# Score products of an item first, transposes three and value products four items behind

## Chip, cores and metric

The kernel runs on one core of one Trainium2 chip. The metric is the device time of one execution in microseconds; the median of 3 runs of the kernel before is 2927.72 us (2925.48 to 2929.70).

## What is computed

One step of a hybrid decoder layer, for a prompt of 2048 tokens and for 8 short sample sequences of 4 tokens with a cache. The change touches the prompt's dilated attention alone. There are 8 heads of 64 dims. Each query attends to itself and 128 keys behind it, in three patterns (stride 1, 4 and 16), and the three outputs are merged afterwards by their log-sum-exp.

```python
# prompt branch for one dilation, cut: 128-query blocks, each against its own and the previous key block
kb = jnp.concatenate([kp[:, :-1], kp[:, 1:]], axis=2)
scores = jnp.einsum('bnqchd,bnkchd->bnchqk', qb, kb).astype(jnp.float32) * (HEAD_DIM ** -0.5)
bias = -slopes[:, None, None] * (dilation * diff).astype(jnp.float32)[None]
scores = jnp.where(valid[None, :, None, None], scores + bias[None, None, None], NEG)
m = jnp.max(scores, axis=-1, keepdims=True)
p = jnp.exp(scores - m)
l = jnp.sum(p, axis=-1, keepdims=True)
out = jnp.einsum('bnchqk,bnkchd->bnqchd', (p / l).astype(v.dtype), vb)
```

Before it come the input projection with norms, after it the output projection, the gated feed-forward part and, beside that, the attention of the samples. All of these are unchanged.

## The kernel before

The program has stages: the input projection of the prompt in 16 tiles of 128 tokens, the prompt attention, the merge with the output projection, and the up and down projections in four chunks of 512 tokens. The attention's first 8 items run at the end of the first stage; the other 184 run in a loop of their own (lines 720 to 739) with an order written out by hand: each engine gets its instructions in the order in which the program issues them.

**An item** is (head h, pattern p, pair pr): two of the 16 query blocks of one head in one pattern. A head has 24 items (3 patterns of 8 pairs). A query block, here called a half of the item, has one or two key blocks of 128: it is 128 or 256 columns wide. Stride 16 has one key block everywhere, stride 4 has two from its fifth query block on, stride 1 from its second. The two items (p, 2n) and (p, 2n+1) come in a row, and the patterns take turns.

**Three steps of an item.** `scores` (line 275) multiplies each half's queries with the keys' high and low parts (lines 289 and 290) into one PSUM bank `Sp`, of which there are four. Then line 292 adds the bias table on VectorE, with the row's minimum into `st` (scores carry a minus sign), and line 294 takes the exponential on ScalarE into `Pt`. `turn` (line 298) transposes the item's two to four blocks of `Pt` on TensorE (line 302) into a PSUM bank `tp` and copies them to `PTs`, three times of four on VectorE (line 305), else on ScalarE (line 307). `values` (line 311) multiplies `PTs` with the values and a column of ones into the bank `Op`, two instructions per block (line 324). Every second item ScalarE copies `Op` to `O` (line 328); after four items of a pattern POOL adds `st` (line 330) and, once both heads of a pair are done, SP stores `O` to DRAM.

**The order.** `advance(i)` (line 356) issues `scores` of item i, `turn` of item i-2 and `values` of item i-3. In `scores` the first half's products, its line 292 and line 294 come ahead of the second half's products. POOL copies queries into the order of a pattern (`spread_q`, line 241) six items ahead.

**Loads.** `load_head` (line 243) loads a head's queries and keys into `QK`, two buffers, in six DMAs of 512 KB on SP's queue (lines 161 to 166), and POOL makes the head's bias table `tab`. It is issued in the loop when item 4 of the head before begins. `next_v` takes one of six `V` buffers, for (pair of heads, pattern, half of the blocks); POOL sets its ones columns (lines 176 and 177) and SP loads it (lines 185 and 193). `NEXT_V` (line 718) says at which items. SP's queue also carries the stores of `O`, small rows of parameters (line 205) and, from item 150 on, eight tiles `rawo` of the output projection's weight (line 737), which ScalarE and VectorE split into a high and a low part (lines 112 and 113).

Of the kernel before, what the change touches and what calls it, by code (L numbers as in the profile page):

```python
# [9 lines left out]
F32 = mybir.dt.float32  # L10
# [7 lines left out]
P = 128  # L18
# [3 lines left out]
H = 8  # L22
# [25 lines left out]
def kernel(ctx, tc, ins, cst, outs):  # L48
# [173 lines left out]
    def store_o(p, hp, O, half):  # L222

        eng = nc.gpsimd if hp == 3 and p == 0 and half else nc.sync
        dst = o_s[p * S:(p + 1) * S, hp, :]
        if p == 0:
            eng.dma_start(dst.rearrange("(n i) f -> i n f", i=P)[:, 8 * half:8 * half + 8], O)
        elif p == 1:
            for J in range(2):
                J2 = 2 * half + J  # L230
                eng.dma_start(dst[J2 * CH:(J2 + 1) * CH].rearrange("(i c) f -> i c f", c=4), O[:, 4 * J:4 * J + 4, :])
        else:
            eng.dma_start(dst.rearrange("(i c) f -> i c f", c=16)[:, 8 * half:8 * half + 8], O)
# [27 lines left out]
    def views(h, p, idx):  # L261
        r = DILS[p]
        blk, c = divmod(idx, r)
        lo = blk - 1 if blk else 0

        def keys(x):
            if p == 0:
                return x[:, lo * P:(blk + 1) * P]
            return x.rearrange("p (m c i) -> p m c i", c=r, i=RUN)[:, lo * P // RUN:(blk + 1) * P // RUN, c, :]

        return queries(h, p, idx), keys(heads[h][1]), keys(heads[h][2]), ([idx - r] if blk else []) + [idx]
# [3 lines left out]
    def scores(it):  # L275
        h, p, pr = it
        tab = heads[h][3]
        if pr % 4 == 0:
            state["st", p] = pq.tile([P, 8], F32, tag="st", name="st", bufs=8)
        st = state["st", p]  # L280
        Sp = psum.tile([P, 2, 2 * P], F32, tag="mm", name="Sp", bufs=4)
        Pt = pq.tile([P, 2, 2 * P], F32, tag="P", name="Pt", bufs=3)
        blocks = []
        for s in range(2):
            idx = 2 * pr + s
            i8 = idx % 8
            q, kh, kl, kb = views(h, p, idx)
            w = P * len(kb)
            nc.tensor.matmul(Sp[:, s, :w], q, kh, start=True, stop=False)  # L289
            nc.tensor.matmul(Sp[:, s, :w], q, kl, start=False, stop=True)  # L290
            T = pq.tile([P, 2 * P], F32, tag="T", name="T", bufs=3)
            nc.vector.tensor_tensor_reduce(out=T[:, :w], in0=Sp[:, s, :w], in1=tab[:, p, 2 * P - w:], op0=ALU.add,  # L292
                                           op1=ALU.min, scale=1.0, scalar=3e38, accum_out=st[:, i8:i8 + 1])
            nc.scalar.activation(Pt[:, s, :w], T[:, :w], AF.Exp, bias=st[:, i8:i8 + 1], scale=-1.0)  # L294
            blocks += [(s, idx % 4, n, b, len(kb)) for n, b in enumerate(kb)]
        return st, Pt, blocks

    def turn(it, res):
        st, Pt, blocks = res
        tp = psum.tile([P, 4, P], F32, tag="tp", name="tp2", bufs=4)  # L300
        for j, (s, i4, n, b, m) in enumerate(blocks):
            nc.tensor.transpose(tp[:, j, :], Pt[:, s, n * P:(n + 1) * P], ident)  # L302
        PT = pq.tile([P, 4, P], F32, tag="PTs", name="PTs", bufs=4)
        if evac[0] % 4:
            nc.vector.tensor_copy(PT[:, :len(blocks)], tp[:, :len(blocks)])
        else:
            nc.scalar.copy(PT[:, :len(blocks)], tp[:, :len(blocks)])
        evac[0] += 1
        return PT

    def values(it, res, PT):
        h, p, pr = it
        hp, h2 = divmod(h, 2)
        st, Pt, blocks = res
        half, pr4 = divmod(pr, 4)
        if h2 == 0 and pr4 == 0 and (p, half) not in pair_o:
            pair_o[p, half] = p2.tile([P, 8, OW], F32, tag="O", name="O", bufs=6)
        O = pair_o[p, half]
        if pr % 2 == 0:
            state["Op", p] = psum.tile([P, 4, DH + 1], F32, tag="tp", name="Op", bufs=4)  # L320
        Op = state["Op", p]
        v0 = h2 * (DH + 1)
        for j, (s, i4, n, b, m) in enumerate(blocks):
            nc.tensor.matmul(Op[:, i4, :], PT[:, j, :], pair_v[hp, p, b][:, v0:v0 + DH + 1],  # L324
                             start=n == 0, stop=n == m - 1)
        o0 = h2 * (DH + 2)
        if pr % 2:
            nc.scalar.copy(O[:, 2 * pr4 - 2:2 * pr4 + 2, o0:o0 + DH + 1], Op)
        if pr4 == 3:
            nc.gpsimd.tensor_copy(O[:, :, o0 + DH + 1], st)  # L330
            if h2 == 1:
                store_o(p, hp, O, half)
                del pair_o[p, half]
# [3 lines left out]
    def turns(seq):  # L337
        at = {}
        for p in seq:
            n = at[p] = at.get(p, -1) + 1  # L340
            yield from ((p, 2 * n), (p, 2 * n + 1))

    ORDER = [(0, 0, 0, 0) + (2, 1) * 4] + [(0, 2, 1) * 4] * (H - 2) + [(0, 2, 2, 1, 2, 0, 2, 1, 0, 1, 1, 0)]
    items = [(h, p, pr) for h in range(H) for p, pr in turns(ORDER[h])]
    NI = 24
    AHEAD = 8
    SPREAD = 6
    attn, PTs = {}, {}

    def spread_next(i):  # L350
        if i < len(items):
            h, p, pr = items[i]
            if p and pr % 2 == 0:
                spread_q(h, p, pr // 2)

    def advance(i):
        if i >= AHEAD:
            spread_next(i + SPREAD)
        if i < len(items):
            attn[i] = scores(items[i])  # L360
        if 0 <= i - 2 < len(items):
            PTs[i - 2] = turn(items[i - 2], attn[i - 2])
        if 0 <= i - 3 < len(items):
            values(items[i - 3], attn.pop(i - 3), PTs.pop(i - 3))


    right = ExitStack()
# [1 line left out]
    with tc.tile_pool(name="p1", bufs=1) as p1:  # L369
# [295 lines left out]
        pq = right.enter_context(tc.tile_pool(name="pq", bufs=1, side="right", reuse_waits="tile"))  # L665
# [17 lines left out]
        for i in range(AHEAD):  # L683
            advance(i)
# [8 lines left out]
    def h_tile(k):  # L693

        return ph.tile([P, 2, TM], F32R, tag=f"h{k}", name="h", bufs=1)
# [14 lines left out]
    with tc.tile_pool(name="p2", bufs=1, reuse_waits="tile") as p2:  # L710
        wo0 = [h_tile(k) for k in range(KT)]
        for half in range(2):
            for p in (2, 1):
                next_v(0, p, half)
        nc.vector.memset(stT[:, :, 2 * SB:], 0.0)
        for i in range(AHEAD, AHEAD + SPREAD):
            spread_next(i)
        NEXT_V = {(1, 14): (2, 0), (1, 17): (0, 0), (1, 21): (1, 0), (1, 23): (0, 1), (0, 1): (2, 1), (0, 3): (1, 1)}

        with tc.manual_schedule():  # L720
            for i in range(AHEAD, len(items) + 3):
                if i < len(items):
                    h, li = divmod(i, NI)
                    if (i == AHEAD or h and li == 4) and h + 1 < H:
                        load_head(h + 1)

                    if (h % 2, li) in NEXT_V and 0 < h < H - (h % 2):
                        next_v((h + 1) // 2, *NEXT_V[h % 2, li])
                    j, r = divmod(i - NI, 8)
                    if r == 0 and 0 <= j < 15:  # L730
                        param_load(j)
                    if r == 5 and 0 < j < 16:
                        param_turn(j - 1)
                    if i >= 150 and i % 5 == 0 and i < 190:
                        k = ((i - 150) // 5 + 4) % KT
                        raw = p2.tile([P, CH], F32, tag="row", name="rawo", bufs=2)
                        nc.sync.dma_start(raw, wov[:, k, 0:CH])
                        split(wo0[k][:, 0, 0:CH], wo0[k][:, 1, 0:CH], raw)
                    if (h, li) == (7, 0):
                        mBs[0] = load_pool(0)  # L740
                advance(i)
# [3 lines left out]
    with tc.tile_pool(name="p4", bufs=1, reuse_waits="tile") as p4:  # L745
# [102 lines left out]
        for gi, grp in enumerate(groups):  # L848
# [22 lines left out]
            for i, t in enumerate(grp):  # L871
# [4 lines left out]
                if i >= late and nxt:  # L876
                    n = nxt[i - late]
# [243 lines left out]
        for c in range(NCHUNK):  # L1121
            last = c == NCHUNK - 1
            T = TM if last else CH
            spans = [(0, T // 2), (T // 2, T // 2)] if last else [(0, CH)]
            nt = 5 if last else 4

            def spread(pss, prompt, sample):

                if not last:
                    return [(prompt, pss[0])]  # L1130
                h = T // 2
                return [(prompt[:, 0:h], pss[0][:, :h]), (prompt[:, h:CH], pss[1][:, :CH - h]),
# [52 lines left out]
            def up_pair(i, slot, act):  # L1185
                gt = conv_tile(i)
                vt = conv_tile(NF + i)
                sg = p4.tile([P, TM], F32, tag="cv", name="sg", bufs=4)
                nc.scalar.activation(sg[:, :T], gt[:, :T], AF.Silu)
                nc.vector.tensor_tensor(out=vt[:, :T], in0=vt[:, :T], in1=sg[:, :T], op=ALU.mult)  # L1190
# [102 lines left out]
```

## Time and profile before

| what | value |
|---|---|
| median of 3 runs | 2927.72 us |
| profiled execution | 2930.08 us |
| its span | 2928.3 us |
| TensorE matmul busy | 2762.1 us (94%) |
| TensorE weight load busy | 2355.7 us (80%) |
| VectorE busy | 1750.5 us (60%) |
| ScalarE busy | 1108.0 us (38%) |
| GpSimd busy | 184.3 us (6%) |
| granted TensorE clock, mean over the span | 0.874 |
| DMA | 393.60 MB, 134 GB/s over the span |

The prompt attention's loop lies between about 466 and 1176 us of the span. In the rows below, PE is TensorE's matmul, PEld its weight load, DVE VectorE, ACT ScalarE, POOL GpSimd; L289 is line 289. Matmuls are pipelined and a row's end is modelled, so the pace of matmuls is read from start to start, not from the length of one row. A few matmul records are missing from a trace. [...]

### The profile page before, as it was taken

Reading aid. Unit: us, or ns where it says so; the run is one execution under the profiler, and the core shown is the slowest. Engines: PE = TensorE matmul, PEld = TensorE weight load, DVE = VectorE, ACT = ScalarE, POOL = GpSimd, SP = SyncE. Lnnn points to the kernel's source line nnn. Section 1 sums busy time; section 2 is a strip of 40 time slices with the busy share of each in tenths; the row PEclk is TensorE's granted clock in tenths of the full one; section 3 lists DMA queues with packets and bytes.
Section 4 is the critical chain, followed back from the end, with each engine's and each line's share of the span. In section 5 each row is a group of like instructions: output and inputs, shape, how many; then the busy total and the mean of one; then the engine's idle time right before and its main releaser. Section 6 shows DMA issues by size and latency. Waiting matters only on the chain.

```text
span 2928.3 us, 36228 instructions
## 1 busy us (share of the span) xinstructions
PE 2762.1 (94%) x13310; PEld 2355.7 (80%) x13310; DVE 1750.5 (60%) x3819; ACT 1108.0 (38%) x2021; POOL 184.3 (6%) x246
## 2 busy tenths in 40 slices
PE   7999997888888687999999999999999999999999
PEld 5888887777777676787788888888888888999998
DVE  6444453333333233676889887888888766666665
ACT  5333333333333233222533434544444444444442
POOL 1111121111011110100000000000000000000000
PEclk9999996555555555999999999999999999999999
DMA  6333335332223411797855565344564344522221
GB/s 201 112 125 112 105 109 146 87 90 45 78 56 81 105 40 37 260 315 251 246 186 176 168 206 183 109 134 144 184 193 129 117 128 140 179 82 87 88 84 58
DMA packets 412877, 393.60 MB, mean 134 GB/s; under 512 B 16347, under 2 KB 319543, under 8 KB 410012
## 3 DMA queue, kind: packets, MB, share of 16 engines
q1 hardware_dynamic: 412476, 390.48, 43.6%
q8 instruction: 105, 1.72, 0.2%
q0 software_dynamic: 224, 0.80, 0.1%
q14 instruction: 72, 0.59, 0.1%
HBM read 305.70 MB, written 85.52 MB: 134 GB/s over the span
## 4 chain that ended last, share of the span: by engine, by line
PE 88%; DVE 4%; issue 3%; DMA 3%; POOL 1%; SPq 0%; ACT 0%; DVEq 0%; POOLq 0%; ACTq 0%
PE pu L1037 34%; PE pd L1213 17%; PE ps L470 11%; PE Op L324 7%; PE po L816 5%; PE Sp L289 5%; PE tp L302 4%; PE Sp L290 3%; DVE T L292 2%; PE tp L122 1%; PE tp L479 1%; PE pd L1207 1%; DMA rawo<-in_w_out_dram 1%; DMA QK<-kT_lo 1%; PE pp L551 0%
## 5 line engine op out<-in xcount | busy, mean ns | idle before, releaser
L1037 PE MATMUL pu<-h,w 128*128 128x512 f32 (+1 forms) x5232 | 990.6, 350 | 2.1 <-ACT w L112 1.6
L1037 PEld LDWEIGHTS pu<-h,w 128*128 128x128 f32 x5232 | 851.0, 188 | 133.4 <-ACT w L112 2.0
L1213 PE MATMUL pd<-w,act 128*128 128x512 f32 x2112 | 490.2, 392 | 0.0
L1213 PEld LDWEIGHTS pd<-w,act 128*128 128x128 f32 x2112 | 396.6, 188 | 88.1
L112 ACT CAST w<-raw 128x1024 fp32r<-128x1024 f32 (+1 forms) x282 | 287.0, 1026 | 292.2 <-PE pd L1213 186.2
L292 DVE CUSTOM_DVE_ANT_0 T<-Sp,tab 128x256 f32<-128x256 f32 (+1 forms) x384 | 140.1, 366 | 421.6 <-PE Sp L290 414.2
L113 DVE TENSOR_TENSOR w<-raw,w 128x1024 fp32r<-128x1024 f32 (+1 forms) x278 | 328.9, 1186 | 24.9 <-ACT w L112 24.8
L470 PE MATMUL ps<-W_hi,xh 128*128 128x512 f32 x1024 | 333.0, 398 | 1.0 <-ACT xh L112 1.0
L294 ACT ACTIVATE Pt<-T,st 128x256 f32<-128x256 f32 (+1 forms) x384 | 176.6, 462 | 411.4 <-DVE st L292 411.4
L1181 DVE SCALAR_TENSOR_TENSOR cv<-ex,cw,cv 128x512 f32<-128x512 f32 x352 | 262.3, 745 | 28.9 <-ACT cv L1173 26.3
L324 PEld LDWEIGHTS Op<-V,PTs 128*128 128x128 f32 x1200 | 273.0, 326 | 0.1
L324 PE MATMUL Op<-V,PTs 128*128 128x65 f32 x1200 | 269.2, 394 | 0.0
L1171 ACT COPY ex<-pu 128x512 f32<-128x512 f32 (+1 forms) x220 | 110.1, 500 | 345.4 <-PE pu L1037 345.2
L470 PEld LDWEIGHTS ps<-W_hi,xh 128*128 128x128 f32 x1024 | 192.7, 189 | 43.2 <-ACT xh L112 1.5
L470 PE MATMUL ps<-W_lo,xh 128*128 128x512 f32 x512 | 202.7, 396 | 0.0
L289 PE MATMUL Sp<-QK,qs 128*128 128x128 f32 (+1 forms) x256 | 128.9, 504 | 74.4 <-DVE st L292 74.4
L1215 DVE TENSOR_TENSOR ya<-ya,pd 128x512 f32<-128x512 f32 x192 | 131.0, 684 | 103.3 <-PE pd L1213 102.6
L95 POOL TENSOR_TENSOR rs<-ms,mhalf 128x8 f32<-128x8 f32 (+3 forms) x68 | 76.4, 1124 | 1588.9 <-DVE stT L1174 1048.8
L302 PE MATMUL tp<-ident,Pt 128*128 128x128 f32 x600 | 166.0, 415 | 0.0
L1173 ACT ACTIVATE cv<-pu,cw 128x512 f32<-128x512 f32 (+3 forms) x264 | 166.0, 649 | 0.0
L289 PEld LDWEIGHTS Sp<-QK,qs 128*128 128x128 f32 x256 | 78.7, 308 | 104.1 <-DVE st L292 103.7
L289 PE MATMUL Sp<-QK 128*128 128x256 f32 (+1 forms) x128 | 69.6, 550 | 61.3 <-DVE st L292 56.7
(225 smaller groups left out, 2905.9 us busy)
## 6 DMA issues: line engine op xcount, KB each, us to landing
raw<-in_w_up_dram SPq DMA_DIRECT2D x176, 512.0 KB
raw<-in_w_down_dram SPq DMA_DIRECT2D x80, 512.0 KB
hn_s<-w SPq DMA_DIRECT2D x16, 1024.0 KB
h<-hn_s SPq DMA_DIRECT2D x32, 512.0 KB
far<-in_cache_k_dram SPq DMA_DIRECT2D x64, 256.0 KB
far<-in_cache_v_dram SPq DMA_DIRECT2D x64, 256.0 KB
om<-o_s SPq DMA_DIRECT2D x16, 792.0 KB
raw<-in_w_in_dram SPq DMA_DIRECT2D x16, 512.0 KB
```

Source lines behind the costliest of these rows:

```text
L112: nc.scalar.copy(hi, src)
L113: (eng or nc.vector).tensor_tensor(out=lo, in0=src, in1=f32(hi), op=ALU.subtract)
L289: nc.tensor.matmul(Sp[:, s, :w], q, kh, start=True, stop=False)
L292: nc.vector.tensor_tensor_reduce(out=T[:, :w], in0=Sp[:, s, :w], in1=tab[:, p, 2 * P - w:], op0=ALU.add, op1=ALU.min, scale=1.0, scalar=3e ...
L294: nc.scalar.activation(Pt[:, s, :w], T[:, :w], AF.Exp, bias=st[:, i8:i8 + 1], scale=-1.0)
L302: nc.tensor.transpose(tp[:, j, :], Pt[:, s, n * P:(n + 1) * P], ident)
L324: nc.tensor.matmul(Op[:, i4, :], PT[:, j, :], pair_v[hp, p, b][:, v0:v0 + DH + 1], start=n == 0, stop=n == m - 1)
L470: nc.tensor.matmul(ps, xh[:, a, k, :], (W_hi, W_lo)[b][j, k // 2][:, k % 2, :], start=n == 0, stop=n == 3 * KT - 1)
L1037: nc.tensor.matmul(ps[:, :n], w[:, a, k, :], hs[k][:, b, c0:c0 + n], start=i == 0, stop=i == 3 * KT - 1)
L1173: nc.scalar.activation(d, s, AF.Identity, bias=cw[:, 3, ct:ct + 1], scale=cw[:, 2, ct:ct + 1])
L1181: nc.vector.scalar_tensor_tensor(out=d, in0=e[j], scalar=cw[:, j, ct:ct + 1], in1=d, op0=ALU.mult, op1=ALU.add)
L1213: nc.tensor.matmul(ps, act[0][:, a, k, tau * P:(tau + 1) * P], wd[k][:, b, :], start=k == 0 and j == 0, stop=k == n - 1 and j == 2)
```

## The change

In `scores`, all four products of an item are issued first, for both halves, and the VectorE and ScalarE steps of the two halves follow. `turn` comes three items behind `scores` in place of two, `values` four in place of three. `Pt` has four buffers in place of three and `PTs` three in place of four. The loop runs one turn longer, and `load_head` and the entries of `NEXT_V` move by one item.

```diff
-        Pt = pq.tile([P, 2, 2 * P], F32, tag="P", name="Pt", bufs=3)
-        blocks = []
+        Pt = pq.tile([P, 2, 2 * P], F32, tag="P", name="Pt", bufs=4)
+        blocks, parts = [], []
         for s in range(2):
             idx = 2 * pr + s
-            i8 = idx % 8
             q, kh, kl, kb = views(h, p, idx)
             w = P * len(kb)
             nc.tensor.matmul(Sp[:, s, :w], q, kh, start=True, stop=False)
             nc.tensor.matmul(Sp[:, s, :w], q, kl, start=False, stop=True)
+            parts.append((s, idx % 8, w))
+            blocks += [(s, idx % 4, n, b, len(kb)) for n, b in enumerate(kb)]
+        for s, i8, w in parts:
             T = pq.tile([P, 2 * P], F32, tag="T", name="T", bufs=3)
             nc.vector.tensor_tensor_reduce(out=T[:, :w], in0=Sp[:, s, :w], in1=tab[:, p, 2 * P - w:], op0=ALU.add,
                                            op1=ALU.min, scale=1.0, scalar=3e38, accum_out=st[:, i8:i8 + 1])
             nc.scalar.activation(Pt[:, s, :w], T[:, :w], AF.Exp, bias=st[:, i8:i8 + 1], scale=-1.0)
-            blocks += [(s, idx % 4, n, b, len(kb)) for n, b in enumerate(kb)]
...
-        PT = pq.tile([P, 4, P], F32, tag="PTs", name="PTs", bufs=4)
+        PT = pq.tile([P, 4, P], F32, tag="PTs", name="PTs", bufs=3)
...
-        if 0 <= i - 2 < len(items):
-            PTs[i - 2] = turn(items[i - 2], attn[i - 2])
         if 0 <= i - 3 < len(items):
-            values(items[i - 3], attn.pop(i - 3), PTs.pop(i - 3))
+            PTs[i - 3] = turn(items[i - 3], attn[i - 3])
+        if 0 <= i - 4 < len(items):
+            values(items[i - 4], attn.pop(i - 4), PTs.pop(i - 4))
...
-        NEXT_V = {(1, 14): (2, 0), (1, 17): (0, 0), (1, 21): (1, 0), (1, 23): (0, 1), (0, 1): (2, 1), (0, 3): (1, 1)}
+        NEXT_V = {(1, 15): (2, 0), (1, 18): (0, 0), (1, 22): (1, 0), (0, 0): (0, 1), (0, 2): (2, 1), (0, 4): (1, 1)}
...
-            for i in range(AHEAD, len(items) + 3):
+            for i in range(AHEAD, len(items) + 4):
...
-                    if (i == AHEAD or h and li == 4) and h + 1 < H:
+                    if (i == AHEAD or h and li == 5) and h + 1 < H:
                         load_head(h + 1)
```

## Rows read from the trace of the kernel before

**Rows 1.** The page's 40 slices of the span, granted TensorE clock in tenths.
```profile
PEclk9999996555555555999999999999999999999999
```
**Rows 2.** Table of stretches: length, busy (instructions) by engine, clock, DMA share, GB/s.
```profile
466.10:1176.10 710.00, 580.42 (x2480) 532.98 (x2480) 222.65 (x898) 224.28 (x516) 85.94 (x148) 0.50 0.28 70
511.00:1022.00 511.00, 420.08 (x1798) 385.29 (x1797) 157.54 (x641) 157.83 (x362) 66.67 (x119) 0.50 0.32 78
```
**Rows 3.** Waits in 466.1 to 1176.1 us: total us, times, longest.
```profile
ACT Pt L294 <- DVE st L292: 397.6, 368, 2.8
...
PE Sp L289 <- DVE st L292: 130.4, 184, 15.1
```
**Rows 4.** Timeline, one item with four blocks: start, us, work, [idle before <- releaser].
```profile
1154.00 0.58 PE L289 MATMUL Sp<-QK,qs 128*128 128x256 f32 x1 [0.62 <-DVE st L292]
...
1154.38 0.42 PE L290 MATMUL Sp<-QK,qs 128*128 128x256 f32 x1
...
1154.60 1.05 PE L302 MATMUL tp<-ident,Pt 128*128 128x128 f32 x4
...
1155.44 1.81 PE L324 MATMUL Op<-V,PTs 128*128 128x65 f32 x8
...
1157.01 0.56 PE L289 MATMUL Sp<-QK,qs 128*128 128x256 f32 x1
...
1157.37 0.41 PE L290 MATMUL Sp<-QK,qs 128*128 128x256 f32 x1
...
1158.42 0.58 PE L289 MATMUL Sp<-QK,qs 128*128 128x256 f32 x1 [0.63 <-DVE st L292]
```
**Rows 5.** Timeline, the scores of an item with 128-wide halves.
```profile
553.86 0.41 PE L290 MATMUL Sp<-QK,qs 128*128 128x128 f32 x1
554.77 0.47 PE L289 MATMUL Sp<-QK,qs 128*128 128x128 f32 x1 [0.50 <-DVE st L292]
555.04 0.41 PE L290 MATMUL Sp<-QK,qs 128*128 128x128 f32 x1
```
**Rows 6.** Groups by form, 466.1 to 1176.1 us: 128-wide first products with spread queries.
```profile
L289 PE MATMUL Sp<-QK,qs 128*128 128x128 f32 x159 | 73.9, 465 | 43.0 <-DVE st L292 43.0
```
**Rows 7.** Timeline at the attention's head: products in a row, low clock.
```profile
446.42 1.19 PE L289 MATMUL Sp<-QK 128*128 128x128 f32 x4 [3.01 <-DMA QK<-kT_hi]
...
450.92 0.41 PE L289 MATMUL Sp<-QK 128*128 128x256 f32 x1
451.14 0.41 PE L290 MATMUL Sp<-QK 128*128 128x256 f32 x1
451.35 1.05 PE L302 MATMUL tp<-ident,Pt 128*128 128x128 f32 x4
```
**Rows 8.** Timeline at the attention's end: the same steps at the high clock.
```profile
1176.45 0.28 PE L290 MATMUL Sp<-QK 128*128 128x256 f32 x1
1176.57 0.60 PE L302 MATMUL tp<-ident,Pt 128*128 128x128 f32 x4
1177.01 1.00 PE L324 MATMUL Op<-V,PTs 128*128 128x65 f32 x8
1177.85 0.60 PE L302 MATMUL tp<-ident,Pt 128*128 128x128 f32 x4
```
**Rows 9.** Table of stretches around the changes of the clock.
```profile
445.70:452.40 6.70, 5.22 (x20) 4.38 (x21) 1.78 (x10) 1.69 (x5) 0.00 (x0) 0.50 1.06 322
452.40:455.90 3.50, 3.50 (x18) 3.29 (x18) 1.46 (x7) 1.80 (x5) 0.00 (x0) 0.50 0.50 158
456.00:461.40 5.40, 5.40 (x51) 5.34 (x48) 3.21 (x13) 3.46 (x8) 2.13 (x11) 1.00 0.76 170
461.40:466.10 4.70, 1.72 (x10) 1.13 (x8) 1.84 (x7) 0.67 (x2) 2.48 (x3) 1.00 0.90 224
1171.70:1176.00 4.30, 4.30 (x18) 4.20 (x19) 0.83 (x4) 1.81 (x4) 0.00 (x0) 0.50 0.02 4
```
**Rows 10.** Timeline of ScalarE: its longest wait in the loop.
```profile
1014.47 0.62 ACT L112 CAST h<-rawo 128x512 fp32r<-128x512 f32 x1 [14.21 <-DMA rawo<-in_w_out_dram]
```

## The prediction

> **What bounds the kernel now.** I read the profile from the top down. The slices come first: the granted TensorE clock is 0.5 in the stretch that holds the prompt attention and 0.9 or more nearly everywhere else [rows 1]. [...] TensorE is busy for 580 us of it, VectorE for 223, ScalarE for 224 and the DMA engines for 0.28 of the time [rows 2]. So TensorE sets the end of this stage, with 130 us of idle time. The waits name all of it: line 289 waits for `st` of line 292, 184 times, which is once per item, 130.4 us in all [rows 3]. The timeline of one item with four blocks shows the place. The second half's first product follows the first half's last product by 1.05 us (1157.37 to 1158.42), because it writes the bank that VectorE is still reading for the first half. Then four transposes and eight value products run with nothing in front of them, up to the next item's first half. The item's period is 4.42 us (1154.00 to 1158.42) [rows 4]. Items with 128-wide halves have the same wait, 0.91 us start to start [rows 5].
>
> **Products first.** Four score products go out with no VectorE step between them. What a product costs without the wait stands at the head of the attention, where the program happened to issue them in a row: 0.22 us for 256 columns and, for 128 columns, (1.19 - 0.47)/3 = 0.24 us [rows 5, 7].
> - 256 wide: 1.05 falls to 0.22, and the step from line 289 to 290 falls from 0.38 to 0.22 [rows 4, 7]: 0.99 us per item.
> - 128 wide: 0.91 falls to 0.24 and 0.27 to 0.24 [rows 5, 7]: 0.70 us per item.
> - Of the 128-wide first products with spread queries there are 159, two per item, so about 80 items [rows 6]; the other 104 of 184 count as wide.
>
> Together 104 x 0.99 + 80 x 0.70 = 159 us at the low clock. Nothing of this is hidden elsewhere: TensorE is the engine that ends last. Of the 130.4 us of idle time about 25 us are other stalls (130.4 - 104 x 0.62 - 80 x 0.50), the longest 15.1 us [rows 3 to 5]; they stay.
>
> **What the first T waits for.** Line 292 of the first half now waits for the second half's two products too, since they write its bank: 0.43 us later. Queued behind it on VectorE are the second T and the eviction of the transposes; behind those, ScalarE's two exponentials. Nobody on TensorE needs them in that item: the transposes take the item three before, the value products the one four before. A whole item (3.4 us at the low clock) lies between. I cost it at nothing; without that cover it is 0.43 x 184 = 79 us.
>
> **The distances and buffers.** `Pt` gets one more buffer and `PTs` one fewer. The slot that an exponential writes was read by transposes one item earlier, as before. The pipeline empties one item later: 0 to 3.4 us, and I take 0, since the next stage's products stand ready in that place. The V loads come one item later and so does their use: nothing. `load_head` comes one item later and its use does not. That moves six 512 KB loads on SP's queue, the table on POOL in front of the query copies, and every load queued behind, `rawo` among them. Bounds: 0 to 3.4 us for each of six heads, 20 us. I take 0 at the low clock, because SP runs ahead of the item loop and a head lasts 93 us (710/7.67). The one stall of this kind, 14.21 us in front of `rawo` behind six QK loads, stays [rows 10].
>
> **The clock.** The low level is the larger prize, and the trace tells how it is left. It rose twice in this mix of work: at 455.9, after 3.5 us in which TensorE was busy for 3.50, and at 1176.0, after 4.3 us with 4.30 busy; the same engine with 5.22 of 6.70 us busy stayed at 0.50. In between it held 1.00 for 5.4 us of attention items without idle time and was lost only after 461.4, when TensorE was busy for 1.72 of 4.70 us [rows 9]. In the 710 us the short wait of each item stands between such stretches. The change takes out just that wait, so I expect the clock to rise early in the stage and to fall only at a long stall.
> The prices at the high level are in the trace: 0.12 us per wide product against 0.22, 0.44 us per four transposes against 0.84, 0.84 us per eight value products against 1.57 [rows 4, 7, 8]: a factor of 0.54. The stage without waits and stalls is 710 - 159 - 25 = 526 us at the low level; times 0.54 that is 284, and with the 25 us of stalls 309 us.
> Then transfers come next. In 511 to 1022 us the DMA engines work 0.32 x 511 = 164 us [rows 2]; at the high level that stretch lasts 511/710 x 309 = 222 us. Three quarters of the time is a tight fit for a queue that issues in order, and QK loads have a fixed deadline per head. The nearest row for one late load is the 14.21 us behind a whole head's QK [rows 10]. I take a third, 5 us, per head, and 5 us more for each stall because the clock drops and comes back only after some 10 us at half pace (445.7 to 455.9) [rows 9]: 10 x 7.67 = 77 us. The bounds are 0 and twice that, 150 us.
> [...]
>
> **The sum.** The profiled execution took 2930.1 us (span 2928.3, 1.8 around it), 2.4 above the median, so I count from it. High clock: 2930 - 710 + 309 + 77 = 2606, less the 2 us to the median: **2604 us**. Its own range is 2527 (no new stall) to 2680 (150 us of them).
>
> **Rivals.**
> - *The clock stays low.* The waits go and nothing else. For it: the clock stayed at 0.50 through 184 items with 2 to 3.6 us of unbroken work in each, and no item with 128-wide halves stands ahead of either rise. Against it: rows 9. Time 2928 - 159 = **2769**, up to 2790 with the 20 us of late QK loads.
> - *The clock comes and goes.* DMA stalls knock it down again and again, and it is up for about half of the work: (2604 + 2769)/2, about **2690**.
> - *Nothing changes.* The order does not do what it says, and the wait reappears in front of the first product or the transposes, at the same length: **2928**. Against: four `Sp` banks are free for four items.
> - *Slower: the ring of `Pt` is one short.* If an exponential had to wait for transposes that themselves stand behind the current item's scores, TensorE would wait in each item for both T chains, 2 x 0.83 us, where it saved 0.86 on average: + 0.8 x 184 = 147 us, **3075**. It decides from a new wait of over 0.86 us (159/184) per item. Against: the slack is one item before and after, and in 368 waits of line 294 the releaser is VectorE alone, never TensorE [rows 3].
>
> **How the numbers follow.** High clock for most of the stage 0.60; comes and goes 0.18; low 0.17; no change 0.02; slower 0.03. The first two hold 0.78, so the range has to reach into the third: 2530 to 2785. A difference of 0.2%, about 6 us, is what a measurement of this kernel can tell from none. Faster by more 0.95, within 0.02, slower 0.03.
>
> **What would show it.** Right: the wait of line 289 for `st` is gone from the waits, the stage's granted clock is near 1, four products stand in a row at 0.12 us. VectorE's T starts only after the fourth product. The waits left in front of TensorE are few and long and lead to a DMA (QK, V, `rawo`), each followed by a piece at 0.5. Wrong on the clock: the stage is dense and still at 0.50, some 550 us long. Wrong on the transfers: the stage is 310 us long, or above 450 at a high clock. Wrong on the whole: transposes or value products show a wait of the item's own length for `Pt` or `PTs`.

## The result

The changed kernel takes 2565.68 us (median of 4 runs, 2562.88 to 2568.02), the kernel before 2926.66 us (4 runs): a ratio of 0.8765, 95% interval 0.875 to 0.878, 361 us less. The forecast was 2604 us, in a range of 2530 to 2785.

The slices of the profile after, granted TensorE clock in tenths (compare [rows 1]):

```profile
PEclk9999999999978999999999999999999999999999
```

The nine slices at 5 are gone. The waits of TensorE in the attention loop, 460.6 to 812.6 us (total us, times, longest; compare [rows 3]). In this kernel the score products stand in lines 288 and 289, the bias step in 294, the exponential in 296, the transposes in 303, their copies in 306 and 308, the value products in 325.

```profile
PE Op L325 <- DVE PTs L306: 31.3, 5, 24.6
PE Sp L288 <- DMA QK<-kT_hi: 6.1, 1, 6.1
PE Op L325 <- ACT PTs L308: 5.9, 14, 1.8
PE Sp L289 <- DMA QK<-kT_lo: 1.9, 1, 1.9
PE tpc L217 <- DMA row<-in_state_ffn_conv_dram: 1.7, 1, 1.7
```

No score product waits for `st`. Of the 46.9 us that are left, 24.6 are one stall, another 4.7 a second one behind the same loads, and 8.0 belong to the first keys of head 1. The table of stretches after (columns as in [rows 2]):

```profile
460.60:812.60 352.00, 304.57 (x2482) 292.45 (x2481) 197.75 (x901) 195.06 (x514) 88.86 (x150) 0.91 0.59 143
498.90:649.00 150.10, 145.81 (x1247) 139.62 (x1246) 95.34 (x442) 94.45 (x250) 43.89 (x79) 1.00 0.68 161
708.70:733.30 24.60, 0.03 (x1) 0.00 (x0) 1.72 (x7) 1.21 (x3) 0.01 (x1) 0.54 0.84 193
819.70:2564.50 1744.80, 1732.76 (x8638) 1457.41 (x8637) 1303.42 (x2400) 709.86 (x1177) 21.40 (x22) 1.00 0.51 161
```

The loop, with the same 2480 or so recorded matmuls, went from 710 to 352 us; its clock is 0.91 in place of 0.50, with a piece of 150 us at 1.00 throughout. From the last value product to the end it is 1744.8 us, against 1746.6 before. So of the 364 us by which the span is shorter, 358 lie in the loop; the other 5.5 lie ahead of it (it begins at 460.6 us in place of 466.1). The scores of an item, in the timeline after (compare [rows 4 and 8]):

```profile
483.36 0.37 PE L288 MATMUL Sp<-QK,qs 128*128 128x256 f32 x1
483.56 0.29 PE L289 MATMUL Sp<-QK,qs 128*128 128x256 f32 x1
483.69 0.28 PE L288 MATMUL Sp<-QK,qs 128*128 128x256 f32 x1
483.80 0.27 PE L289 MATMUL Sp<-QK,qs 128*128 128x256 f32 x1
483.92 0.38 PE L303 MATMUL tp<-ident,Pt 128*128 128x128 f32 x2
...
484.22 0.42 DVE L294 CUSTOM_DVE_ANT_0 T<-Sp,tab 128x256 f32<-128x256 f32 x1 [0.42 <-PE tp L303]
```

Four products take 0.56 us (483.36 to 483.92), and the first bias step starts only after the fourth of them, at 484.22.

### The profile page after: what moved, and what is told of

Same layout as the page of the kernel before. It is cut to its first block, busy times and chain, and to the rows that moved or that the text cites. A ratio compares the mean times of both kernels' runs of the same rounds, so it can differ in the third digit from the quotient of the medians.

```text
span 2564.5 us, 35986 instructions
## 1 busy us (share of the span) xinstructions
PE 2483.7 (97%) x13310; PEld 2113.6 (82%) x13310; DVE 1724.9 (67%) x3819; ACT 1078.5 (42%) x2021; POOL 185.9 (7%) x246
## 4 chain that ended last, share of the span: by engine, by line
PE 66%; DMA 1%; DVE 1%; issue 0%; ACT 0%; SPq 0%; POOL 0%; DVEq 0%; ACTq 0%; POOLq 0%
PE pu L1038 38%; PE pd L1214 19%; PE po L817 5%; PE pd L1208 1%; PE tp L122 0%; DMA raw<-in_w_out_dram 0%; PE Op L325 0%; DMA h<-hn_s 0%; DMA raw<-in_w_up_dram 0%; PE sacc L990 0%; PE sacc L989 0%; PE po L1071 0%; DVE at L796 0%; PE tpa L802 0%; DMA om<-o_s 0%
## 5 line engine op out<-in xcount | busy, mean ns | idle before, releaser
L296 ACT ACTIVATE Pt<-T,st 128x256 f32<-128x256 f32 (+1 forms) x384 | 157.0, 456 | 137.4 <-DVE st L294 136.7
L294 DVE CUSTOM_DVE_ANT_0 T<-Sp,tab 128x256 f32<-128x256 f32 (+1 forms) x384 | 125.3, 364 | 122.0 <-PE Sp L289 93.3
L325 PE MATMUL Op<-V,PTs 128*128 128x65 f32 x1200 | 167.1, 278 | 38.1 <-DVE PTs L306 31.3
L325 PEld LDWEIGHTS Op<-V,PTs 128*128 128x128 f32 x1200 | 155.9, 199 | 48.7 <-DVE PTs L306 33.9
L112 ACT CAST act<-cv 128x512 fp32r<-128x512 f32 x88 | 54.6, 621 | 159.4 <-DVE cv L1191 152.6
L471 PEld LDWEIGHTS ps<-W_lo,xh 128*128 128x128 f32 x512 | 96.7, 189 | 19.9
L1175 DVE COPY stT<-ex 128x2 f32<-128x2 f32 x176 | 28.8, 163 | 117.1 <-ACT ex L1172 117.0
L303 PE MATMUL tp<-ident,Pt 128*128 128x128 f32 x600 | 102.9, 284 | 0.0
```

The lines of the kernel that those rows point to most:

```text
L112: nc.scalar.copy(hi, src)
L471: nc.tensor.matmul(ps, xh[:, a, k, :], (W_hi, W_lo)[b][j, k // 2][:, k % 2, :], start=n == 0, stop=n == 3 * KT - 1)
```

## Experiments

**Which part does it.** The first run takes the product order alone, the second the distances alone.

```diff
# e1_products_only: the kernel before, but in scores
+            parts.append((s, idx % 8, w))
+        for s, i8, w in parts:
             T = ...            # bias step and exponential of both halves, after all four products
# e2_distance_only: the changed kernel, but in scores the bias step and the exponential
# stand inside the loop over the halves, as before
```

> The kernel before with one part of the change: the four products of an item first. Distances (two and three), buffers and the places of the loads as before. Theory A (the wait between the two halves' products holds the clock down, and taking it out is the whole gain): the granted clock of the attention loop rises to 0.9 or more, the loop falls from 710 to some 350 to 380 us, 2566 to 2600 us. Theory B (the longer distances are needed, since transposes two items behind then wait for their exponentials): a new wait of line 302 for line 294 appears, 0.2 to 0.6 us per item, the clock stays at 0.50, 2770 to 2830 us.

> The changed kernel with the old order inside scores: distances three and four, buffers and loads as changed, but each half's bias step and exponential stand right behind its two products. Theory A: the wait of line 289 for st stays at about 130 us, the clock at 0.50, the time within 6 us of the 2927 before. Theory B (the distances bring the gain): 2566 to 2700 us.

The first takes 2564.59 us, ratio 0.8757 (0.8744 to 0.877), the whole gain; the second 2929.03 us, ratio 1.0004 (0.9994 to 1.0013), nothing that can be measured. Loop and waits of the first, then of the second:

```profile
461.50:811.00 349.50, 303.80 (x2479) 293.65 (x2479) 197.90 (x900) 195.03 (x514) 88.01 (x149) 0.91 0.60 144
PE Op L325 <- ACT PTs L308: 30.7, 16, 25.4
PE Op L325 <- DVE PTs L306: 9.1, 5, 5.1
```

```profile
466.70:1176.20 709.50, 580.36 (x2481) 532.76 (x2481) 223.12 (x897) 223.14 (x514) 85.75 (x148) 0.50 0.29 70
PE Sp L289 <- DVE st L292: 130.1, 184, 18.6
```

With distances of two and three no transpose waits for its exponential, so theory B falls on both sides. The longer distances, the buffers and the moved loads are worth nothing measurable.

**Is it the order of the products, or the idle time?** In the kernel before, the transposes and value products were put between the two halves, so that the bias step runs behind them. Inside an item the two halves' products are apart; the second half's products and the next item's first ones now follow each other, in two banks.

```diff
             nc.scalar.activation(Pt[:, s, :w], T[:, :w], AF.Exp, bias=st[:, i8:i8 + 1], scale=-1.0)
+            if s == 0:
+                between()      # turn of item i-2, values of item i-3; in advance they are gone
```

> The kernel before in everything but the order on the queues: transposes and value products stand between the first and the second half's products, so that the bias step of the first half runs behind them. Distances two and three, buffers and loads as before. Theory A (idle time on TensorE is what counts, in whatever way it is filled): the wait for st is nearly gone, the clock rises, 2566 to 2640 us. Theory G (four products in a row are needed for the clock): clock 0.50, only the waits' 105 us saved, 2800 to 2825 us.

2573.32 us, ratio 0.8792 (0.8779 to 0.8806). Loop and waits:

```profile
462.70:828.40 365.70, 322.36 (x2487) 313.39 (x2488) 206.23 (x897) 204.20 (x516) 87.30 (x148) 0.87 0.56 137
PE Sp L289 <- DVE st L292: 35.9, 9, 22.9
PE Sp L289 <- DMA QK<-kT_hi: 3.4, 1, 3.4
```

The 184 waits have become 9, and the clock is up. Theory A holds: another filling of the same gap gives nearly the same time. Theory G, by which four products in a row are needed, does not fall by this run: four still stand in a row, two of one item and two of the next.

```profile
561.55 0.36 PE L289 MATMUL Sp<-QK 128*128 128x256 f32 x1
561.76 0.28 PE L290 MATMUL Sp<-QK 128*128 128x256 f32 x1
561.88 0.23 PE L289 MATMUL Sp<-QK,qs 128*128 128x128 f32 x1
561.95 0.27 PE L290 MATMUL Sp<-QK,qs 128*128 128x128 f32 x1
```

The run e8_transposes_between, below, settles it.

**How much idle time holds the clock down.** Two runs leave part of it in: the whole wait in every second item, and a shortened wait in each item whose transposes do not cover it.

```diff
# e3_every_second_item: the changed kernel
+            if pr % 2 == 0:
+                finish(parts.pop())    # bias step and exponential at once, as before
+        for part in parts:
+            finish(part)
# e8_transposes_between: the kernel before
+            if s == 0:
+                between()              # turn of item i-2 only; values stay behind the scores
```

> The changed kernel with the old order inside scores in every first item of a pair, so that the wait between the halves stands in 92 items of 184. Theory C (one short wait in some 7 us is enough to hold the clock down): clock 0.50, half of the wait's price back, 2771 + 80 = 2850 us. Theory D (what counts is how much the engine stands idle over some time, and half of the waits leaves enough work): the clock is up for most of the loop, the waits cost 92 x 0.8 = 74 us on top, 2640 us.

> The kernel before with only the transposes between the first and the second half's products. They take 0.42 to 0.84 us at the low clock against a chain of 0.83 us, so an item keeps a wait of 0 to 0.4 us at the low clock and 0.4 to 0.6 us at the high one, in every item. Theory D (what counts is how much the engine stands idle over some time): about the same idle sum as with a whole wait in every second item, where the clock was up for 0.58 of the loop; 2640 to 2720 us. Theory H (a wait in every item keeps the clock low, however short): clock 0.50, two thirds of the waits' 105 us saved, 2840 to 2870 us.

2657.81 us for the first, ratio 0.9074 (0.9056 to 0.9092), and 2701.97 us for the second, ratio 0.92 (0.9142 to 0.9258). First the loop of every second item, two stretches of it, and its waits; then the loop and waits of the other:

```profile
461.70:919.70 458.00, 373.32 (x2479) 354.10 (x2479) 209.37 (x899) 204.76 (x514) 86.81 (x149) 0.79 0.45 109
581.00:620.00 39.00, 35.50 (x163) 33.90 (x162) 13.25 (x55) 13.09 (x32) 5.46 (x8) 0.50 0.19 41
624.60:730.30 105.70, 88.56 (x734) 83.14 (x734) 58.26 (x256) 56.50 (x145) 25.95 (x44) 1.00 0.59 137
PE Sp L296 <- DVE st L288: 84.7, 92, 22.9
```

```profile
464.30:947.00 482.70, 419.64 (x2480) 372.63 (x2481) 215.25 (x897) 219.28 (x516) 86.76 (x148) 0.74 0.42 103
PE Sp L289 <- DVE st L292: 59.8, 99, 21.5
```

Theory C, by which one short wait in some 7 us is enough to hold the clock down, falls. With half of the waits the clock is at the high level for somewhat more than half of the loop (0.79 is 58% at 1.00 and 42% at 0.50, worked out with the two levels that its stretches show), and it is not even: the same order of work runs 39 us at 0.50 and right behind that 106 us at 1.00. The idle time in a stretch does not tell the two apart: TensorE was busy for 35.50 of 39.00 us at the low clock, for 88.56 of 105.70 at the high one. This is what the rival "the clock comes and goes" describes, with short waits in place of its DMA stalls.

Theory H speaks of a wait in every item, and the second run does not test it as it stands: only 99 of the 184 items wait. Theory G falls by this run. No more than two score products stand in a row in it, between transposes and value products, and the clock was 1.00 for 92 us on end:

```profile
528.00:620.00 92.00, 81.72 (x620) 70.45 (x619) 52.39 (x220) 52.23 (x124) 23.15 (x41) 1.00 0.52 126
541.19 0.28 PE L290 MATMUL Sp<-QK,qs 128*128 128x128 f32 x1
541.30 0.62 PE L304 MATMUL tp<-ident,Pt 128*128 128x128 f32 x4
542.00 0.33 PE L289 MATMUL Sp<-QK,qs 128*128 128x128 f32 x1
542.17 0.28 PE L290 MATMUL Sp<-QK,qs 128*128 128x128 f32 x1
542.28 1.05 PE L326 MATMUL Op<-V,PTs 128*128 128x65 f32 x8
```

**The stall that is left.** The changed kernel's longest wait, in its timeline: SP's loads, ScalarE, VectorE and TensorE.

```profile
712.91 0.60 SPq L161 DMA_DIRECT2D QK<-qT_hi  x1
717.05 15.57 SPq L738 DMA_DIRECT2D rawo<-in_w_out_dram  x3
730.93 0.62 ACT L112 CAST h<-rawo 128x512 fp32r<-128x512 f32 x1 [23.63 <-DMA rawo<-in_w_out_dram]
731.58 0.69 DVE L113 TENSOR_TENSOR h<-rawo,h 128x512 fp32r<-128x512 f32 x1 [24.83 <-ACT h L112]
733.35 1.12 PE L325 MATMUL Op<-V,PTs 128*128 128x65 f32 x4 [24.62 <-DVE PTs L306]
```

The item loop reached the split at about 707 us. SP, which issued its loads in the order of the program, came to the last head's QK loads only at 712.9 and to `rawo` at 717.0. ScalarE's split waits for `rawo`, and the exponentials are queued behind it; VectorE's part of the split waits for ScalarE, and the copies of the transposes stand behind that; TensorE then waits for a copy. The two runs move the load.

```diff
# e4_rawo_early: load at i = 145, 150, ..., split five items later, at i = 150, 155, ...
# e6_rawo_late: load at i = 159, 162, ..., split six items later, at i = 165, 168, ...
-                        nc.sync.dma_start(raw, wov[:, k, 0:CH])
-                        split(wo0[k][:, 0, 0:CH], wo0[k][:, 1, 0:CH], raw)
+                        split(wo0[k][:, 0, 0:CH], wo0[k][:, 1, 0:CH], raws.pop(k))
+                        nc.sync.dma_start(raws[k], wov[:, k, 0:CH])      # a later k
```

> The changed kernel with each rawo tile loaded five items ahead of its split, ahead of the last head's QK loads in SP's queue. The changed kernel stood still for 24.6 and 4.7 us behind rawo and ran some 12 us at the low clock right after. Theory E (these stalls set the end): both go, with half of the low stretches, 2566 - 29 - 6 = 2531 us. Theory F (the QK or V transfers behind them are late anyway): the stall comes back in front of a product of head 7 or of the values, 2555 to 2566 us.

> The changed kernel with rawo split from item 165 on in steps of three and loaded six items ahead, so that the first one is issued ten items behind the last head's QK loads. Loading five items ahead from item 145 on had left one stall of 15.4 us, since the second tile was issued right behind those loads. Theory E (the rawo stalls are paid in full): no stall over 2 us behind rawo, 24.6 + 4.7 us and some 10 us of the low clock's price go, 2525 to 2540 us. Theory F (the QK loads of head 7 are late anyway): the stall shows up in front of head 7's queries or products, 2550 to 2566 us.

The early load takes 2554.52 us, ratio 0.8722 (0.8709 to 0.8735): only part of it. The first tile came in time; the second, issued right behind the QK loads, did not:

```profile
714.30 0.59 SPq L166 DMA_DIRECT2D QK<-kT_lo  x1
714.99 1.00 SPq L742 DMA_DIRECT2D rawo<-in_w_out_dram  x2
...
729.99 0.62 ACT L112 CAST h<-rawo 128x512 fp32r<-128x512 f32 x1 [15.83 <-DMA rawo<-in_w_out_dram]
```

The late split takes 2529.50 us, ratio 0.8642 (0.8629 to 0.8655), 36 us less than the change alone and the fastest version with the next one. Its loop and waits:

```profile
464.00:779.00 315.00, 302.95 (x2486) 290.47 (x2487) 197.88 (x901) 194.79 (x514) 88.96 (x150) 0.96 0.65 160
PE Op L325 <- ACT PTs L308: 5.4, 15, 0.8
PE Op L325 <- DVE PTs L306: 5.2, 6, 1.3
```

So both stalls behind `rawo`, 24.6 and 4.7 us, are gone, and nothing behind them was late. The 36 us are not theirs alone: the 8.0 us of waits for head 1's keys are gone in this run too, at the price of 24 us at the low clock in head 0, as the next run's paragraph shows.

**Head 1's keys earlier.**

```diff
             for p in (2, 1):
                 next_v(0, p, half)
+            if half == 0:
+                load_head(1)
```

> As the run before this one, and the QK loads of head 1 are issued between the two halves of the first pair's V loads, ten V DMAs earlier in SP's queue. Theory E: the two waits for head 1's keys, 6.1 and 1.9 us in the changed kernel, go, with some 4 us of the low clock's price; 10 to 12 us under the run before this one. Theory F (the V loads that now come later are waited for): values of items 16 on wait for their V tile, no gain or a loss of some us.

2528.31 us, ratio 0.8639 (0.8626 to 0.8652): no difference from the run before it. It settles nothing, since the wait that it should remove was not there in that run either: head 0 ran at the low clock for 24 us in both profiled executions (0.50 and 0.51), and the load was done in time. The stretch in e6_rawo_late:

```profile
461.70:485.60 23.90, 22.62 (x108) 22.50 (x108) 8.58 (x43) 8.09 (x22) 7.12 (x9) 0.50 0.69 172
```

## Why the prediction held, step by step

**What bounds it.** Right. The wait between the two halves' products is the cause: taking it away by the order of products (e1_products_only) or by filling it (e5_steps_between) gives the gain, and keeping it with all the rest of the change (e2_distance_only) gives none.

**The first T waits for four products.** Right in the main, but not at nothing. Outside the two stalls behind `rawo`, value products wait for `PTs` for 7.9 us, in 17 places, where the kernel before has its idle time in front of score products alone [rows 3]. The cover was reckoned as an item of 3.4 us at the low clock; at the high one an item lasts 288/184 = 1.6 us on average. In 14 of the 17 places the late copy is ScalarE's; the one at 473.24 us stands behind two exponentials, as the prediction had the queue. With the shorter distances it was much the same.

**Distances, buffers, moved loads.** Right at nothing. No exponential waits for a transpose, so the `Pt` ring was never short and the slower rival did not come up.

**The clock.** Right in its direction and in its prices. The chain of the argument was: short waits stand between stretches of unbroken work, both rises follow such stretches [rows 9], so without the waits the clock rises. By the numbers after, the loop's work without waits and at the high level is 352.0 - 46.9 (waits) - 17 = 288 us, where the sum had 284. The 17 is an estimate, worked out from the mean clock and the levels 0.50 and 1.00: 0.91 means 63 us at the low level, some 27 of them inside the long stall and the two waits for head 1's keys; the other 36 us of work cost 0.46 of that, by the factor 0.54. The rival by which the clock stays low is out. Transposes among the products did not hold the clock down: 150 us with transposes in every item (498.9 to 649.0) were granted 1.00.

How the 358 us of the loop split between the waits and the clock was not measured by itself, since no run here took the waits away and kept the low clock for a whole loop. By the prices of the prediction it is 159 for the waits and some 200 for the clock. The price of a wait can be checked in one item after, behind the long stall, where the clock is 0.50:

```profile
734.22 0.45 PE L288 MATMUL Sp<-QK,qs 128*128 128x128 f32 x1
734.48 0.41 PE L289 MATMUL Sp<-QK,qs 128*128 128x128 f32 x1
734.69 0.41 PE L288 MATMUL Sp<-QK,qs 128*128 128x128 f32 x1
734.90 0.41 PE L289 MATMUL Sp<-QK,qs 128*128 128x128 f32 x1
```

From the second product to the fourth it is 0.42 us, where the kernel before took 1.18 (553.86 to 555.04) [rows 5]: 0.76 less, for a price of 0.70 in the sum.

**The transfers.** This is the term that was mis-sized. The sum had 25 us of old stalls and 77 us for late loads and the clock's falls behind them, 102 in all; measured are 46.9 and 17, that is 64. With the 4 us of work more, that is the 34 us by which the loop's 352 stayed under the forecast 386; the 5.5 us ahead of the loop stood in no term. I had one late load per head. The keys came late once, for head 1 (6.1 and 1.9 us); for heads 2 to 7 no product waited for keys, at 0.68 of DMA time in the dense stretch. In place of that the old `rawo` stall, which I had kept at its old size, grew from 15.1 to 24.6 us, because the items now overtake SP's queue. It grew as much with `load_head` at its old place (25.4 us in e1_products_only), so the moved load is not the cause.

## What to carry to other kernels

Here the granted clock was 0.50 through a whole stage, and the short waits in it were worth more than their own length: 130 us of idle time was all that the waits showed, and 361 us came back. In such a stage look for an engine that reads half of a PSUM bank while TensorE has the other half still to write, and put all of a bank's products ahead of its readers, or other work of TensorE between them. After such a gain read the long waits anew: a load that was in time at the old pace (head 1's keys) was late by 6.1 and 1.9 us at the new one, and one that was late (`rawo`, 15.1 us) was later (24.6 us), and stood in front of everything in its consumer's queue.

## What was not expected of the hardware

One order of work ran at both levels of the clock. In e3_every_second_item, with a wait of 0.68 us on average in every second item, (84.7 - 22.9)/91, it ran at 0.50 for 39 us and at 1.00 for 106 us. Four of its five runs spread from 2649.58 to 2672.60 us, where those of the changed kernel lie within 5.2 us; the fifth took 2718.12 us. The kernel before, with a wait in every item, stayed at 0.50 for 710 us [rows 2, 3].

Unbroken work did not raise it at once everywhere: in e6_rawo_late TensorE was busy for 22.62 of 23.90 us in head 0 at 0.50, where the changed kernel had 1.00 from 451.2 to 488.6 us. From 466 to 481 us all halves of its items were 128 wide, and the clock rose at about 485.5 us, behind two items with 256-wide halves. Whether the kind of work counts beside the idle time, no run here separates, and what sets the moment stays open.
